# Where the sample's memory attention runs: from the gate units to a third stream beside the prompt's dilated attention

## The chip, the cores and the metric

The kernel runs on one core of a Trainium2 chip. The metric is the device time of one execution in microseconds. TensorE is PE in the views, its weight loads are PEld, VectorE is DVE, ScalarE is ACT, GpSimd is POOL, and SyncE (SP) issues nearly all DMA transfers from one queue.

## The reference, cut to what matters

One layer of a decoder step over a prompt of 1024 tokens and 8 samples of 4 new tokens each. One input projection is split into three groups of heads: retention, dilated sliding-window attention with a rotary embedding, and cross-attention into 256 memory tokens. Each group has a gate; the gated groups go through one output projection and a layer norm. All is fp32. The change touches the memory attention of the samples only:

```python
def _mem_attn(q, k, v):     # q (8, 4 tokens, 4 heads, 128), k and v (8, 256, 4, 128)
    s = jnp.einsum('bthd,bmhd->bhtm', q, k).astype(F32) * (MEM_HD ** -0.5)
    p = jax.nn.softmax(s, axis=-1)
    return jnp.einsum('bhtm,bmhd->bthd', p, v.astype(F32))
```

Each sample has its own `k` and `v` (`cache_mem_k`, `cache_mem_v`, 512 KB each), so sixteen transfers of 512 KB belong to this part.

## The kernel before, in words

The order of the work on every engine is the order in which the program emits it. The trunk of it is a loop over 22 units of the input projection (`UNITS`), two to each name from `mq` to `sg`: memory queries `mq`, memory keys and values `mk` and `mv`, dilated queries and keys `qk`, values `vr`, retention `rq` and `rk`, then the gates `rg`, `mg` and `sg`. A unit takes four blocks of weights (`wr`, 256 KB each); ACT makes the high half `wh` (L172) and DVE the low half `wl` (L175). Its parts are 24 matmuls at L224 each, three (high by high, high by low, low by high) for each of 8 blocks of the contraction, into one tile of the pool `ps_p` (three buffers). Units with the rotary embedding (`qk`, `rq`, `rk`) hold two of these tiles at a time, which DVE and POOL then read.

Between the matmuls, four times in a part, `pump` gives credit to three streams of other work: `fa` (the prompt's attentions), `fb` (the sample's dilated attention) and `fc` (retention, and the sample's memory attention). The table `RATE` holds the credit of each stream by unit. A stream with a whole credit runs its generator to its next `yield`, so what stands there between two yields goes into the program as one piece between two projection matmuls. `drain` runs a stream to its end without any projection between.

In `vr1` to `vr3` (units `vr` 1, `qk` 2, `vr` 2, `rk`, `qk` 3, `vr` 3) `fa` runs the prompt's dilated attention: score matmuls at L523 on `q` and `k` that are read back from memory (`q<-hl_d`), a row operation on DVE (L525), the exponential on ACT (L531), transposes (L573), values (L602). In the rotary units DVE multiplies the projection's tile with a table (L276).

The sample's memory attention is `mem_sample` (L893 to L974). It is added to `fc` when the sample's retention has ended, at the start of `sg` 0, in memory that the retention gave back. It loads `k` tiles (`kv<-in_mem_kT`) into a ring of nine buffers, builds masked queries `msq` (POOL clears them, ACT copies into them), and computes scores in four steps (L930, two samples of different groups of 32 partitions in turns, eight matmuls on 32 columns, one `ps_t` tile for all). A softmax follows, two transposes (L950), four value steps (L960, all in one `ps_o` tile), a product with `own_h` (L964) and a sum (L967) on DVE, a transpose (L970), and a store of `msu` to memory, which the output stage reads as part of the mixed features (`mraw`, times the gate `mg`).

In the second half of `sg` 1 (`MIX_AT`) the program drains `fc`, closes the memory of `mem_sample`, and opens the pools of the output stage there, whose first loads follow. L1498 are the output projection's matmuls. The sample's dilated attention (`fb`) runs in `mg` and `sg`; `dn<-in_swa_kd` (L1058) and the tiles `cl` are its loads. L881 belongs to the sample's retention.

Of the kernel before, what the change touches and what calls it, by code (L numbers as in the profile page):

```python
# [42 lines left out]
MS_Y = 5  # L43
# [26 lines left out]
GT_DEFER = 14  # L70
RT_DEFER = 10
# [26 lines left out]
def trunk_kernel(ctx: ExitStack, tc: tile.TileContext, d):  # L98
# [794 lines left out]
    def mem_sample():  # L893
        kb, vb = {}, {}
        pairs = ((0, 2), (4, 6), (1, 3), (5, 7))
        due = deque((kind, b) for kind in "kv" for pair in pairs for b in pair)

        def load_next():
            if due:
                kind, b = due.popleft()  # L900
                t = msp.tile([128, 1024], F32, tag="kv", name="kv", bufs=9)
                if kind == "k":
                    kb[b] = t.rearrange("p (h m) -> p h m", h=4)
                    load(kb[b], d["mem_kT"][b])
                else:
                    vb[b] = t.rearrange("p (m f) -> p m f", m=2)
                    load(vb[b], d["mem_v"][b])
# [4 lines left out]
        for _ in range(4):  # L912
            load_next()
# [9 lines left out]
        for _ in range(1 + MS_Y):  # L923
            yield
# [18 lines left out]
        for _ in range(2):
            load_next()
            load_next()
            yield
# [8 lines left out]
        o = ps_o.tile([128, 512], F32, tag="o", name="o")  # L955
        for n, pair in enumerate(pairs):
            for mt in range(2):
                for b in pair:
                    g, y = divmod(b, 2)
                    nc.tensor.matmul(o[32 * g:32 * g + 32], lhsT=pm[:, mt, g, y].rearrange("p y r -> p (y r)"), rhs=vb[b][:, mt],  # L960
                                     start=(y == 0 and mt == 0), stop=(y == 1 and mt == 1))
# [787 lines left out]
```

## Time and profile before

| | |
|---|---|
| runs shown | 902.46, 905.25, 922.29 us (median 905.25) |
| profiled execution | 902.89 us, span on the core 901.1 us |
| mean granted clock of TensorE | 0.978 |
| DMA packets | 160.92 MB, mean 179 GB/s |
| chain that ended last | PE 67%, DMA 17%, DVE 5%, SP's queue 4%, ACT 3% |

Times in the rows are microseconds from the start of the span unless they are marked ns. A row of the timeline gives start, duration, engine, line, operation, tile written and tile read, a count, and in brackets how long the engine had stood idle and what ended that. A row of the waits gives the engine, the tile and line that waited, what released it, and the sum, the count and the longest. The granted clock is a share of 2.4 GHz: 0.50 is 1.2 GHz. An fp32 matmul has two records, a matmul of the split halves one.

### The profile page before, as it was taken

What the parts mean: (1) busy time and instruction counts of PE and PEld (TensorE: products, weight loads), DVE (VectorE), ACT (ScalarE), POOL (GpSimd) and SP (SyncE); (2) the same over time, 40 slices, a digit from 0 to 9 for tenths busy, and PEclk for the clock granted to TensorE, in tenths of its full rate; (3) what the DMA queues carried; (4) which work ended last, traced back from release to release, by engine and by line L of the source; (5) the groups of instructions that cost most, each with busy time, mean ns of one, the idle gap of its engine ahead of it and who ended that gap; (6) DMA issues with size and microseconds to landing.
All of it is one profiled execution on the core that took longest, in us unless ns stands there. A gap on an engine that the chain in (4) does not pass through costs nothing.

```text
span 901.1 us, 16168 instructions
## 1 busy us (share of the span) xinstructions
PE 847.5 (94%) x6034; PEld 756.6 (84%) x6034; DVE 456.3 (51%) x1048; ACT 310.4 (34%) x863; POOL 245.7 (27%) x249
## 2 busy tenths in 40 slices
PE   7999999999998999989999999989898889899996
PEld 6999999998997999989998878878775767677776
DVE  5656345145435533555245453585575458545425
ACT  5545234243434433433344444433111442100000
POOL 0004023015123331335012130358450305322201
PEclk9999999999999999999999999999899999899999
DMA  8574324775647544545683326768984868869631
GB/s 262 178 205 140 120 93 130 199 176 108 150 110 160 160 125 133 148 121 126 168 211 84 83 74 208 247 207 294 356 293 151 252 231 241 271 215 307 239 110 56
DMA packets 141646, 160.92 MB, mean 179 GB/s; under 512 B 39232, under 2 KB 102592, under 8 KB 141568
## 3 DMA queue, kind: packets, MB, share of 16 engines
q1 hardware_dynamic: 141568, 159.89, 60.6%
q8 instruction: 48, 0.79, 0.4%
q14 instruction: 30, 0.25, 0.1%
HBM read 120.59 MB, written 39.26 MB: 177 GB/s over the span
## 4 chain that ended last, share of the span: by engine, by line
PE 67%; DMA 17%; DVE 5%; SPq 4%; ACT 3%; issue 2%; POOL 1%; POOLq 0%; DVEq 0%; ACTq 0%
PE pp L224 35%; PE pp L1498 9%; PE s L523 4%; PE o L602 3%; DMA q<-hl_d 3%; SPq L162 3%; DMA wr<-in_w_out 2%; DMA s<-in_xT 2%; DMA dn<-in_swa_kd 2%; PE tp L573 1%; DVE wl L175 1%; PE s L1172 1%; DMA gt_d<-t 1%; PE o L436 1%; PE s L399 1%
## 5 line engine op out<-in xcount | busy, mean ns | idle before, releaser
L224 PE MATMUL pp<-xh,wh 128*128 128x352 f32 x672 | 230.5, 343 | 5.7 <-ACT xh L172 5.3
L224 PE MATMUL pp<-xh,wl 128*128 128x352 f32 x672 | 220.7, 328 | 0.0
L224 PE MATMUL pp<-xl,wh 128*128 128x352 f32 x672 | 220.6, 328 | 0.0
L224 PEld LDWEIGHTS pp<-xh,wh 128*128 128x128 f32 x672 | 130.4, 194 | 16.5 <-issue 9.2
L175 DVE TENSOR_TENSOR wl<-wr,wh 128x512 fp32r<-128x512 f32 (+1 forms) x113 | 91.8, 821 | 87.7 <-ACT wh L172 87.2
L224 PEld LDWEIGHTS pp<-xl,wh 128*128 128x128 f32 x672 | 130.5, 194 | 0.7 <-DVE xl L175 0.5
L224 PEld LDWEIGHTS pp<-xh,wl 128*128 128x128 f32 x672 | 129.8, 193 | 0.3 <-DVE wl L175 0.3
L563 POOL TENSOR_TENSOR pt<-pt,sf 128x256 f32<-128x256 f32 (+1 forms) x128 | 71.3, 593 | 146.2 <-DVE sf L556 130.6
L531 ACT ACTIVATE pt<-pt,sw 128x256 f32<-128x256 f32 (+1 forms) x128 | 59.6, 467 | 83.3 <-DVE sw L525 80.4
L1498 PE MATMUL pp<-wh,mh 128*128 128x512 f32 x192 | 78.9, 411 | 7.7 <-ACT wh L172 6.4
L172 ACT ACTIVATE wh<-wr 128x512 fp32r<-128x512 f32 (+1 forms) x113 | 69.3, 622 | 26.6 <-DMA wr<-in_w_out 22.1
L1498 PE MATMUL pp<-wl,mh 128*128 128x512 f32 x192 | 77.4, 403 | 0.6 <-DVE wl L175 0.5
L1498 PE MATMUL pp<-wh,ml 128*128 128x512 f32 x192 | 77.0, 401 | 0.1
L224 PE MATMUL pp<-wh,xh 128*128 128x256 f32 x256 | 75.0, 293 | 0.5 <-ACT t L172 0.5
L224 PE MATMUL pp<-wl,xh 128*128 128x256 f32 x256 | 72.2, 282 | 0.0
L224 PE MATMUL pp<-wh,xl 128*128 128x256 f32 x256 | 72.0, 281 | 0.0
L523 PE MATMUL s<-k,q 128*128 128x256 f32 (+1 forms) x256 | 56.0, 354 | 12.8 <-DMA q<-hl_d 10.6
L525 DVE CUSTOM_DVE_ANT_0 pt<-s,mask 128x256 f32<-128x256 f32 (+1 forms) x128 | 43.3, 379 | 48.4 <-PE s L523 40.6
L523 PEld LDWEIGHTS s<-k,q 128*128 128x128 f32 x256 | 50.5, 260 | 14.9 <-DVE t L279 5.9
L1071 POOL TENSOR_TENSOR cl<-cl,qb 128x1536 f32<-128x1536 f32 x16 | 56.4, 3542 | 20.2 <-DMA cl<-in_swa_kc 11.2
L1498 PEld LDWEIGHTS pp<-wh,mh 128*128 128x128 f32 x192 | 36.9, 192 | 20.0 <-ACT wh L172 7.7
L1225 POOL TENSOR_TENSOR mraw<-mraw,mg 128x512 f32<-128x512 f32 (+1 forms) x27 | 41.0, 1536 | 45.3 <-DMA mg<-gt_d 44.8
(238 smaller groups left out, 1421.0 us busy)
## 6 DMA issues: line engine op xcount, KB each, us to landing
wr<-in_w_in SPq DMA_DIRECT2D x87, 256.0 KB, 4.0
cl<-in_swa_kc SPq DMA_DIRECT2D x16, 768.0 KB, 6.5
cl<-in_swa_vc SPq DMA_DIRECT2D x16, 768.0 KB, 6.3
hl_d<-hl SPq DMA_DIRECT2D x24, 352.0 KB, 2.9
q<-hl_d SPq DMA_DIRECT2D x32, 256.0 KB, 5.2
tab<-in_tabs SPq DMA_DIRECT2D x18, 352.0 KB, 3.4
gt_d<-t SPq DMA_DIRECT2D x36, 176.0 KB, 5.0
wr<-in_w_out SPq DMA_DIRECT2D x24, 256.0 KB, 5.5
```

The lines of the kernel that those rows point to most:

```text
L162: nc.sync.dma_start(out=out, in_=in_)
L172: nc.scalar.activation(out=out, in_=in_, func=copy, **kw)
L175: (nc.gpsimd if pool else nc.vector).tensor_tensor(out=out, in0=raw, in1=hi.bitcast(F32), op=ALU.subtract)
L224: nc.tensor.matmul(out, lhsT=a, rhs=b, start=(n == 0), stop=(n == 3 * KD - 1))
L523: nc.tensor.matmul(ps[:, out], lhsT=Q[h, b][:, x, q], rhs=K[h][:, k], start=(x == 0), stop=(x == 1))
L525: nc.vector.tensor_tensor_reduce(out=pt[:, out], in0=ps[:, out], in1=mask[:, msk], scale=1.0, scalar=3.0e38, op0=ALU.add, op1=ALU.min, acc ...
L531: nc.scalar.activation(out=pt[:, out], in_=pt[:, out], func=exp, scale=-1.0, bias=st[:, s, i, 0:1], accum_out=st[:, s, i, 1:2])
L563: nc.gpsimd.tensor_tensor(out=pt[:, out], in0=pt[:, out], in1=f[:, 0, 4 * s + i, None].to_broadcast([128, n]), op=ALU.mult)
L602: nc.tensor.matmul(o[64 * g:64 * g + 64, col:col + 128], lhsT=v, rhs=pt[:, at:at + 128], start=g not in begun, stop=last and final[g] == n)
L1071: product(n, K_POOL)(out=pr, in0=pr, in1=qb_t[b][:, None, :].to_broadcast([128, 3, 512]), op=ALU.mult)
L1225: nc.gpsimd.tensor_tensor(out=raw, in0=raw, in1=g, op=ALU.mult)
L1498: nc.tensor.matmul(ps, lhsT=a[:, k], rhs=b[k, c], start=(n == 0), stop=(n == 35))
```

## The change

`mem_sample` is added to `fc` at the start of `vr` 1 (`MS_AT`), with a rate of 0.35 in the six units `vr` 1 to `vr` 3, and `fc` is drained at the start of `rg` 0, where its memory is closed. The memory lies on the other side, above the pool of the rotary tables. The ring has three buffers in place of nine: three tiles are loaded ahead, then two after each step, one yield later. The pair of a step are samples `2g` and `2g+1`, whose results lie in the same 32 partitions, in place of `(0,2)`, `(4,6)`, `(1,3)`, `(5,7)` with results in two groups of 32. Each step has a tile of `ps_p` of its own, which ACT copies out (scores) or DVE multiplies out with `own_h` (values, one operation of 32 partitions for each step). `to_mem`, now `after_rs`, opens nothing any more; `fc.drain()` in `sg` 1 stays.

```diff
+MS_AT = ("vr", 1)
...
-    ("vr", 0): (0.8, 0), ("rq", 0): (0.95, 0), ("vr", 1): (0.65, 0), ("qk", 2): (0.95, 0), ("vr", 2): (0.8, 0), ("rk", 0): (0.7, 0),
...
+    ("vr", 0): (0.8, 0), ("rq", 0): (0.95, 0), ("vr", 1): (0.65, 0, 0.35), ("qk", 2): (0.95, 0, 0.35), ("vr", 2): (0.8, 0, 0.35), ("rk", 0): (0.7, 0, 0.35),
...
     def mem_sample():
-        kb, vb = {}, {}
-        pairs = ((0, 2), (4, 6), (1, 3), (5, 7))
-        due = deque((kind, b) for kind in "kv" for pair in pairs for b in pair)
+        due = deque((kind, b) for kind in "kv" for b in range(8))
+        held = {}
...
-                t = msp.tile([128, 1024], F32, tag="kv", name="kv", bufs=9)
...
+                t = msp.tile([128, 1024], F32, tag="kv", name="kv", bufs=3)
...
-        ps = ps_t.tile([128, 512], F32, tag="t", name="tp")[:, 0:256]
-        for n, pair in enumerate(pairs):
-            for h in range(4):
-                for b in pair:
-                    g, y = divmod(b, 2)
-                    nc.tensor.matmul(ps[32 * g:32 * g + 32], lhsT=qm[:, g, y, h].rearrange("p y h t -> p (y h t)"), rhs=kb[b][:, h],
+        for g in range(4):
+            r = slice(32 * g, 32 * g + 32)
+            ps = ps_p.tile([128, 512], F32, tag="p", name="pp")[r, 0:256]
+            for y in range(2):
+                k = held.pop(("k", 2 * g + y)).rearrange("p (h m) -> p h m", h=4)
+                for h in range(4):
+                    nc.tensor.matmul(ps, lhsT=qm[:, g, y, h].rearrange("p y h t -> p (y h t)"), rhs=k[:, h],
                                      start=(y == 0 and h == 0), stop=(y == 1 and h == 3))
+            acopy(p[r], ps)
             yield
             load_next()
             load_next()
             yield
...
+        for g in range(4):
+            r = slice(32 * g, 32 * g + 32)
+            o = ps_p.tile([128, 512], F32, tag="p", name="pp")[r]
...
+                for mt in range(2):
+                    nc.tensor.matmul(o, lhsT=pm[:, mt, g, y].rearrange("p y r -> p (y r)"), rhs=v[:, mt],
                                      start=(y == 0 and mt == 0), stop=(y == 1 and mt == 1))
...
+            nc.vector.tensor_tensor(out=u4[r], in0=o.rearrange("p (h e) -> p h e", h=4),
+                                    in1=own_h[r, :, None].to_broadcast([32, 4, 128]), op=ALU.mult)
+            yield
+            load_next()
+            load_next()
+            yield
...
+        if (kind, j) == MS_AT:
+            ms_es = ExitStack()
+            msp = pool(ms_es, "msp", 1, side="right")
+            fc.add("ms", mem_sample())
         if (kind, j) == ("rg", 0):
+            fc.drain()
+            close(ms_es)
             close(rope_es)
...
             if u + 1 == len(UNITS) and n == MIX_AT:
                 fc.drain()
-                close(ms_es)
```

PE's order, a score step. Before, in `sg` 0, between projection matmuls of the gate; the numbers behind the names are those of the tiles:

```order
L224 MATMUL pp_7586<-xh_145,wl_7417 128x352
L930 MATMUL tp_7625<-kv_7461,msq_7471 32x256
L930 MATMUL tp_7625<-kv_7463,msq_7471 32x256
L930 MATMUL tp_7625<-kv_7461,msq_7471 32x256
L930 MATMUL tp_7625<-kv_7463,msq_7471 32x256
L930 MATMUL tp_7625<-kv_7461,msq_7471 32x256
L930 MATMUL tp_7625<-kv_7463,msq_7471 32x256
L930 MATMUL tp_7625<-kv_7461,msq_7471 32x256
L930 MATMUL tp_7625<-kv_7463,msq_7471 32x256
L224 MATMUL pp_7634<-xh_145,wh_7103 128x352
```

And now, in `vr` 1:

```order
L224 MATMUL pp_2980<-wh_2369,xh_145 128x256
L224 MATMUL pp_2980<-wl_2370,xh_145 128x256
L224 MATMUL pp_2980<-wh_2369,xl_146 128x256
L929 MATMUL pp_2998<-kv_2783,msq_2791 32x256 x4
L929 MATMUL pp_2998<-kv_2785,msq_2791 32x256 x4
L224 MATMUL pp_2980<-wh_2505,xh_145 128x256
L224 MATMUL pp_2980<-wl_2506,xh_145 128x256
```

The two `kv` tiles no longer take turns, and the step stands in the middle of a projection part, in a tile of that part's pool.

PE's order, the value steps. Before, in the drain of `sg` 1:

```order
L224 MATMUL pp<-xl,wh 128x352
L224 MATMUL pp<-xh,wl 128x352
L950 MATMUL tp<-ident,msp 128x128 x2
L960 MATMUL o<-kv,mspm 32x512 x16
L970 MATMUL tp<-ident,msu_7922 128x128
L224 MATMUL pp<-xh,wh 128x352
L224 MATMUL pp<-xl,wh 128x352
```

And now one of the four, in `rk`:

```order
L224 MATMUL pp_4338<-xl_146,wh_4080 128x352
L224 MATMUL pp_4338<-xh_145,wl_4081 128x352
L959 MATMUL pp_4370<-kv_3678,mspm_2793 32x512 x2
L959 MATMUL pp_4370<-kv_4303,mspm_2793 32x512 x2
L224 MATMUL pp_4338<-xh_145,wh_4195 128x352
L224 MATMUL pp_4338<-xl_146,wh_4195 128x352
```

Sixteen value matmuls in one piece with a transpose ahead and one behind have become four pieces of four, each between projection matmuls.

SP's queue around the loads of `q` in `qk` 2. Before:

```order
L162 DMA so<-st_d_0_97 128x8
L162 DMA k<-hl_d_82 64x1024 x2
L162 DMA q<-hl_d_82 64x2x512 x2
L162 DMA wr<-in_w_in 128x512
L537 DMA st_d_0_99<-sw 128x4x2
L537 DMA st_d_1_100<-sw 128x8
L162 DMA tab<-in_tabs 128x704
```

And now:

```order
L162 DMA k<-hl_d_82 64x1024 x2
L162 DMA q<-hl_d_82 64x2x512 x2
L162 DMA kv<-in_mem_kT 128x1024
L162 DMA kv<-in_mem_v 128x1024
L162 DMA wr<-in_w_in 128x512
L537 DMA st_d_0_99<-sw 128x4x2
L537 DMA st_d_1_100<-sw 128x8
L162 DMA tab<-in_tabs 128x704
```

Two of the sixteen `kv` loads stand directly behind the `q` loads; the first of them is a `k` tile of the fourth score step.

## Rows read from the trace of the kernel before

**Rows 1.** The page's first part, busy time of each engine with its share of the span and the count of instructions.

```profile
PE 847.5 (94%) x6034; PEld 756.6 (84%) x6034; DVE 456.3 (51%) x1048; ACT 310.4 (34%) x863; POOL 245.7 (27%) x249
```

**Rows 2.** Busy time by stage: the stretch, its length, busy us (instructions) of PE, PEld, DVE, ACT and POOL, the granted clock, the DMA share and GB/s. First `vr` 1 to `vr` 3, then `sg` 0 and `sg` 1.

```profile
221.00:448.00 227.00, 220.39 (x1660) 205.74 (x1659) 103.64 (x334) 86.29 (x278) 66.91 (x104) 0.98 0.54 139
634.00:711.00 77.00, 68.33 (x413) 55.58 (x413) 44.67 (x62) 20.02 (x58) 28.29 (x13) 0.93 0.78 262
```

**Rows 3.** The waits of PE from 221 to 448, the heaviest: us, times, longest.

```profile
PE s L523 <- DMA q<-hl_d: 5.8, 2, 3.5
```

**Rows 4.** Records of matmuls. The first three rows group by line and form: duration of one record in ns, shortest, median and longest, and where they lie. The last is four transposes in the timeline.

```profile
L930 PE MATMUL tp<-kv,msq x64: 379/379/603, 653.0 to 674.1; 128*32 128x256 f32 x64
L960 PE MATMUL o<-kv,mspm x32: 592/592/617, 683.4 to 691.1; 128*32 128x512 f32 x32
L573 PE MATMUL tp<-ident,pt x120: 270/272/421, 207.7 to 537.2; 128*128 128x128 f32 x120
210.45 0.60 PE L573 MATMUL tp<-ident,pt 128*128 128x128 f32 x4
```

**Rows 5.** The timeline of PE around one score step in `sg` 0.

```profile
660.46 0.32 PE L224 MATMUL pp<-xl,wh 128*128 128x352 f32 x1
660.62 0.32 PE L224 MATMUL pp<-xh,wl 128*128 128x352 f32 x1
660.87 1.92 PE L930 MATMUL tp<-kv,msq 128*32 128x256 f32 x16
662.72 0.43 PE L224 MATMUL pp<-xh,wh 128*128 128x352 f32 x1
```

**Rows 6.** The timeline of PE and DVE around the drain in `sg` 1.

```profile
681.08 0.32 PE L224 MATMUL pp<-xh,wl 128*128 128x352 f32 x1
...
683.38 2.76 PE L960 MATMUL o<-kv,mspm 128*32 128x512 f32 x18
...
686.84 2.74 PE L960 MATMUL o<-kv,mspm 128*32 128x512 f32 x8 [0.71 <-DMA kv<-in_mem_v]
...
691.75 0.69 DVE L964 TENSOR_TENSOR msu<-o,own_h 128x512 f32<-128x512 f32 x1 [8.54 <-PE o L960]
692.48 1.02 DVE L967 TENSOR_REDUCE msu<-msu 128x128 f32<-128x512 f32 x1
693.64 0.30 PE L970 MATMUL tp<-ident,msu 128*128 128x128 f32 x1 [1.93 <-DVE msu L967]
693.70 0.40 PE L224 MATMUL pp<-xh,wh 128*128 128x352 f32 x1
```

**Rows 7.** Four stretches at half clock, with columns as in rows 2.

```profile
615.90:619.30 3.40, 3.40 (x16) 3.40 (x14) 1.94 (x2) 1.10 (x4) 3.21 (x2) 0.51 0.98 346
646.60:653.40 6.80, 4.85 (x24) 3.87 (x26) 2.60 (x3) 0.62 (x2) 4.87 (x2) 0.50 1.04 353
694.40:697.80 3.40, 3.40 (x14) 3.40 (x13) 2.26 (x5) 0.00 (x0) 0.00 (x0) 0.50 0.15 24
721.70:725.10 3.40, 3.26 (x8) 2.42 (x8) 2.36 (x4) 1.93 (x4) 0.00 (x0) 0.50 0.53 170
```

**Rows 8.** The start of `sg` 0: two rows of PE's timeline, one of SP's, and one of the chain of waits (start, duration).

```profile
644.21 0.32 PE L224 MATMUL pp<-xh,wl 128*128 128x352 f32 x1
...
648.55 0.66 PE L1058 MATMUL sd<-dn,qbd 128*32 128x128 f32 x8 [4.02 <-DMA dn<-in_swa_kd]
...
635.65 1.84 SPq L162 DMA_DIRECT2D kv<-in_mem_kT  x4
...
638.85 9.56 DMA dn<-in_swa_kd
```

**Rows 9.** Loads in the dilated stage: timelines of SP and PE in `qk` 2 and `qk` 3; then the landing of the sixteen `kv` loads in `sg` 0 and 1, and the page's row on the `q` loads (count, KB each, median us to landing).

```profile
281.76 1.25 SPq L162 DMA_DIRECT2D q<-hl_d  x2
283.12 0.54 SPq L162 DMA_DIRECT2D wr<-in_w_in  x1
...
288.22 1.19 PE L523 MATMUL s<-k,q 128*128 128x128 f32 x4 [3.51 <-DMA q<-hl_d]
289.70 0.64 PE L224 MATMUL pp<-xh,wh 128*128 128x352 f32 x1
...
386.59 0.73 PE L523 MATMUL s<-k,q 128*128 128x256 f32 x4 [2.31 <-DMA q<-hl_d]
...
DMA to landing us min/median/max: 4.2/6.8/9.7
...
q<-hl_d SPq DMA_DIRECT2D x32, 256.0 KB, 5.2
```

**Rows 10.** DVE's operation on the projection tile of a rotary unit, grouped by line: ns, and where they lie.

```profile
L276 DVE TENSOR_TENSOR raw<-pp,tab x18: 511/519/527, 67.4 to 417.6; 128x352 f32<-128x352 f32 x18
```

**Rows 11.** The timeline of PE at two places: ahead of the stretch from 615.9, and at the first matmuls of the output projection.

```profile
613.34 1.97 PE L881 MATMUL tp<-rv 32*64 32x128 f32 x16 [1.77 <-ACT rv L172]
...
721.40 0.59 PE L1498 MATMUL pp<-wh,mh 128*128 128x512 f32 x1 [4.93 <-ACT wh L172]
```

**Rows 12.** The waits of SP's queue from 628 to 712, two of them: us, times, longest.

```profile
SPq L151 <- ACT msu L172: 9.5, 1, 9.5
SPq L162 <- DMA ut_d<-msu: 2.4, 1, 2.4
```

More of the change, by code (lines that the diff above doesn't have):

```diff
@@ L42 @@
 RL = 3
-MS_Y = 5
 V_Y = 3
@@ L900, in load_next @@
                 kind, b = due.popleft()
-                t = msp.tile([128, 1024], F32, tag="kv", name="kv", bufs=9)
[L902 to L907, printed above, removed]
+                t = msp.tile([128, 1024], F32, tag="kv", name="kv", bufs=3)
+                load(t.rearrange("p (h m) -> p h m", h=4) if kind == "k" else t.rearrange("p (m f) -> p m f", m=2),
+                     d["mem_kT" if kind == "k" else "mem_v"][b])
+                held[kind, b] = t
         def one(shape, name):
             return msp.tile(shape, F32, name=name)
-        for _ in range(4):
+        for _ in range(3):
             load_next()
@@ L922, in mem_sample @@
                 acopy(qm[:, :, y, h, y, h], mq_s[:, h].rearrange("p (g y t) -> p g y t", y=2, t=4)[:, :, y])
-        for _ in range(1 + MS_Y):
-            yield
-        ps = ps_t.tile([128, 512], F32, tag="t", name="tp")[:, 0:256]
-        for n, pair in enumerate(pairs):
-            for h in range(4):
-                for b in pair:
-                    g, y = divmod(b, 2)
-                    nc.tensor.matmul(ps[32 * g:32 * g + 32], lhsT=qm[:, g, y, h].rearrange("p y h t -> p (y h t)"), rhs=kb[b][:, h],
+        yield
+        p = one([128, 256], "msp")
+        st = stat.tile([128, 16], F32, tag="st", name="st")
+        for g in range(4):
[5 more added lines that the diff above has]
+                    nc.tensor.matmul(ps, lhsT=qm[:, g, y, h].rearrange("p y h t -> p (y h t)"), rhs=k[:, h],
                                      start=(y == 0 and h == 0), stop=(y == 1 and h == 3))
+            acopy(p[r], ps)
             yield
@@ L935, in mem_sample @@
             yield
-        st = stat.tile([128, 16], F32, tag="st", name="st")
-        nc.vector.tensor_reduce(out=st[:, 0:1], in_=ps, axis=AX.X, op=ALU.max)
+        nc.vector.tensor_reduce(out=st[:, 0:1], in_=p, axis=AX.X, op=ALU.max)
         nc.vector.tensor_scalar(out=st[:, 1:2], in0=st[:, 0:1], scalar1=-MEM_SCALE, scalar2=None, op0=ALU.mult)
-        p = one([128, 256], "msp")
-        nc.scalar.activation(out=p, in_=ps, func=exp, scale=MEM_SCALE, bias=st[:, 1:2], accum_out=st[:, 2:3])
+        yield
+        nc.scalar.activation(out=p, in_=p, func=exp, scale=MEM_SCALE, bias=st[:, 1:2], accum_out=st[:, 2:3])
         nc.vector.reciprocal(out=st[:, 3:4], in_=st[:, 2:3])
         nc.vector.tensor_scalar(out=p, in0=p, scalar1=st[:, 3:4], scalar2=None, op0=ALU.mult)
[L943 to L946, printed above, removed]
+        yield
         yield
@@ L954, in mem_sample @@
         yield
[L955 to L960, printed above, removed]
+        u4 = one([128, 4, 128], "msu4")
+        for g in range(4):
+            r = slice(32 * g, 32 * g + 32)
+            o = ps_p.tile([128, 512], F32, tag="p", name="pp")[r]
+            for y in range(2):
+                v = held.pop(("v", 2 * g + y)).rearrange("p (m f) -> p m f", m=2)
+                for mt in range(2):
+                    nc.tensor.matmul(o, lhsT=pm[:, mt, g, y].rearrange("p y r -> p (y r)"), rhs=v[:, mt],
                                      start=(y == 0 and mt == 0), stop=(y == 1 and mt == 1))
+            nc.vector.tensor_tensor(out=u4[r], in0=o.rearrange("p (h e) -> p h e", h=4),
+                                    in1=own_h[r, :, None].to_broadcast([32, 4, 128]), op=ALU.mult)
             yield
-        u4 = one([128, 4, 128], "msu4")
-        nc.vector.tensor_tensor(out=u4, in0=o.rearrange("p (h e) -> p h e", h=4),
-                                in1=own_h[:, :, None].to_broadcast([128, 4, 128]), op=ALU.mult)
+            load_next()
+            load_next()
+            yield
         u1 = one([128, 128], "msu1")
         nc.vector.tensor_reduce(out=u1, in_=u4.rearrange("p h e -> p e h"), axis=AX.X, op=ALU.add)
+        yield
         yield
@@ L1409, in trunk_kernel @@
             close(swa_es)
-            ret_es, cl_es, ms_es = ExitStack(), ExitStack(), ExitStack()
+            ret_es, cl_es = ExitStack(), ExitStack()
             sw1 = pool(cl_es, "sw1", 1)
```

7 lines of the change are left out of this document (2 added, 5 removed), and 2 rows, old and new, of the table RATE.

## The prediction, before the changed kernel had run

> **What bounds the kernel now.** I read the page's busy shares first: TensorE (PE) is busy for 847.5 us of 901.1, and no other engine for more than 456 us [rows 1]. So time can be lost or won in PE's stream, or where PE stands. I then read a table by stage [rows 2]. In 221:448, where the prompt's dilated attention runs beside the projections, PE is busy for 220.4 of 227 us, the DMA share is 0.54 and the rate 139 GB/s. In 634:711 (the gate units `sg0` and `sg1`, where the memory attention of the sample stands) PE is busy for 68.3 of 77 us, the clock is 0.93, and the rate 262 GB/s. The waits of PE in 221:448 name one releaser of weight, the `q` loads, 5.8 us in two waits [rows 3]. The reader is to see that the stage which receives the work has hardly a hole to put it in, while the stage that gives it up has holes.
>
> **What leaves the gate units.** Four score steps: between the L224 matmul before one and the next L224 stand 660.62 + 0.16 (the spacing of L224) to 662.72, that is 1.94 us [rows 5], four times 7.8 us. Then the drain: the last L224 starts at 681.08, the next at 693.70 [rows 6], so 12.5 us hold no projection; in them PE waits for the `v` tiles and for the two DVE operations of 0.69 and 1.02 us. Together 20.3 us. With them go three losses that I tie to this work. After the drain the clock stands at 0.50 from 694.4 to 697.8 [rows 7], where 3.4 us do the work of 1.7. At 644.21 PE waits 4.02 us for a `dn` tile whose load took 9.56 us, issued just after four `kv` loads [rows 8]; and the clock is at 0.50 from 646.6 to 653.4 [rows 7], which costs 3.4 us. 1.7 + 4.0 + 3.4 = 9.1 us. Gone from the gates: 29.4 us.
>
> **What arrives in the dilated stage.** First the price of one step, which is no longer what it was. Before, one score step alternates two samples whose outputs lie at different partitions (groups 0 and 1, or 2 and 3); its 8 matmuls are 16 records. A record of 256 columns lasts 379 ns and one of 512 lasts 592 [rows 4], so 256 columns more take 213 ns; four full-width transposes of 128 columns last 0.60 us, which is a spacing of (0.60 - 0.27)/3 = 109 ns, the same rate [rows 4]. At that rate 16 records after one another would last 15 x 0.213 + 0.379 = 3.58 us. They last 1.92 [rows 5]: two ran side by side. After the change both samples of a step write the same 32 partitions, so nothing runs beside anything: a score step is 1.94 + (3.58 - 1.92) = 3.60 us, a value step of 8 records 7 x 0.427 + 0.592 = 3.58, with the same edges 3.60. Eight steps are 28.8 us; three transposes in two bursts add about 0.9 (an estimate from 0.30 for L970 [rows 6] and the edges). 29.7 us arrive, and since PE there is dense, I count all of it. Both sides so far: 29.7 - 29.4 = +0.3 us.
>
> New waits in the dilated stage, each bounded:
> - The projection pool `ps_p` has three tiles, and a rope unit holds two. At three steps (the third score step in `qk2`, the second value step in `rk`, the last in `qk3`) the step takes the third, and the next half of a rope part then waits for two DVE operations of 0.52 us on the older tile [rows 10]. 0 to 3 x 1.04 = 3.1 us; I take 2, as other PE work stands between at one of them.
> - The fourth score step needs a `k` tile whose load now stands in SP's queue directly behind two `q` loads for which PE already waits 3.51 us, until 288.22 [rows 9]. Issued near 283.1 (where `wr` went out) and landing after 6.8, at most 9.7 us [rows 9], it is there between 289.9 and 292.8; PE asks at 289.7. 0 to 3.1, I take 2.
> - Loads one stream yield ahead of use (at the second value step 24 L224 matmuls lie between, in the order, at a spacing of 0.16 some 4 us of PE's time; at the second score step about the same), against 4.2 us for the quickest landing and 6.8 for the median [rows 9]: 0 to 2.6 each, I take 1 for both, since the first tile of a pair was fetched a step earlier.
> - The second `q` wait near 384 gets one more load of 512 KB in front: 0 to 3, I take 1.
> - What queues behind a late step: ACT's copy of the scores, and on DVE L961 (four of 0.69 at most, against one now), are on nobody's path, because projection tiles rotate through three buffers. POOL's two memsets go from the gates, where POOL waited before them, to `vr1`. The added SP issues (half a microsecond each) hide under PE.
> - Clock: every stretch at 0.50 costs 1.7 us. A step of 3.6 us in which only 32 columns work may be followed by one: 615.9 to 619.3 is such a stretch [rows 7], and what preceded it is 16 narrow matmuls of L881 in 1.97 us after a wait of 1.77 [rows 11]; the earlier narrow steps of 1.92 us had none. 0 to 8 x 1.7 = 13.6; I take one, 1.7, since projections at full width surround each step. The Trainium skill ("TensorE: Matmul & The Clock Gate", Part 1) says that the throttled clock is the default and that a busy array releases it. By that rule alone a step without a hole costs no clock, and this term would be 0; the stretch after L881 leaves it open, because a wait stood there too.
>
> In the gates, with PE's cover gone:
> - DVE is busy for 44.7 us of 77 in 634:711 [rows 2]. Without the memory attention's DVE work (about 2.5) it has 42 us to do while PE's own need shrinks to 77 - 29.4 = 47.6. DVE also waits there for POOL's products, so it may hold projection tiles. 0 to 6, I take 2.
> - SP stood 9.5 us for the result `msu` and 2.4 for its landing before it could fetch `mraw` [rows 12]; PE's later wait of 4.93 us for weights at 721.40 follows from that queue [rows 11]. The mix loads reuse the memory of the `kv` tiles, so both waits go. A gain of 0 to 4.9 + 1.7 (the stretch at 721.7 [rows 7]); I take 2, as those weights also queue behind the mixes and the value cache.
>
> Sum: 0.3 + 2 + 2 + 1 + 1 + 1.7 + 2 - 2 = +8.0 us. The profiled execution took 902.9 us, the median of the runs shown is 905.25. 902.9 + 8 = 911, and with the median's offset 913: I say 912 us.
>
> **Rivals.**
> - *The gates win more than they lose elsewhere.* For it: DMA is at 0.78 in 634:711, and SP's two waits for `msu` stand ahead of the weights. If no new wait comes in the dilated stage and the weights' wait goes with its stretch of clock, the sum is 0.3 - 4.9 - 1.7 = -6.3: 897 us. Against it: 16 loads of 512 KB into a stage where PE already stands for `q`.
> - *A new wait in place of the old, slower than before.* Mechanism: the `kv` tiles (three buffers, two refilled at once) arrive late in the dilated stage, PE stands in the step, and the clock falls after it. Place: the four steps whose second tile is fetched one yield ahead. Price: 2.6 us (median landing less the 4 us of distance) plus 1.7 us for each, 4.3 x 4 = 17, less the 5 us of such waits and clock already in the sum: 912 + 12 = 924, and with a stretch of half clock after the other steps too up to 931. It decides from a landing of about 5 us on. For it: `q` lands in 5.2 us in the median and `kv` in up to 9.7 [rows 9]. Against: at 139 GB/s the stage has room.
> - *The change doesn't double PE's time for a step.* If records to the same 32 partitions overlap after all, the eight steps cost what they did, 13.3 us less: 899. Against it: the spacing of the transposes. The Trainium skill ("TensorEngine Tiling (Array Packing)", Tiling Modes, Key Properties) says that different tiles of the array execute in parallel, and so nothing for two matmuls in one tile; by it this rival is out, and the rows of the alternating step, 1.92 against 3.58, agree.
>
> **How the numbers follow.** Forecast 0.60; gates win 0.18; late tiles 0.17; no doubling 0.05. The likeliest time is 912. Its bounds are 897 (all terms at their low ends with the weights' gain) and 931 (late tiles with clock). From 897 to 930 leaves out about one in ten above and one below. A measurement of this kernel tells some 2% from no change, that is 887 and 923. Below 887 lie only a corner of the second case and of the fourth, 0.04; above 923 most of the late tiles and a corner of the forecast, 0.16; the rest, 0.80, is within.
>
> **What would show it.** Right: L929 bursts of 16 records lasting 3.5 to 3.7 us, L959 bursts of 8 the same; 634:711 shrunk to 47 to 52 us from the first `sg0` matmul to the last of `sg1`; no wait of PE for `dn` near `sg0`; the stage from `vr1` to `vr3` longer by 33 to 40. Wrong: steps of 1.9 us (no doubling); a long PE wait for `kv` in the waits of the dilated stage, or more than three new stretches at half clock (the late tiles); PE standing for DVE in `sg0` (the gates give back what they won); a time under 897 would mean that the transition into the output projection lost its waits altogether.

## The result, and the profile after

The changed kernel took 913.11 us in the median of four runs (910.88 to 914.71), the kernel before 903.86 us on the same chip (four runs); the ratio is 1.0104, 95% interval 1.0057 to 1.0151. Timed once more on another chip it was 1.0114 (1.0075 to 1.0153). It is slower by about one per cent, 9 to 10 us, inside the range of 897 to 930. The prediction took 2% as the least that a measurement of this kernel tells from no change; here the two intervals leave 1 out at half of that. Only runs within 1.5% of the fastest of their kernel enter ratios and means (922.29 us of the kernel before and two runs of `no_mem` at 886 us do not). Chips differ: the median of the kernel before lay between 901.5 and 906.1 us from batch to batch, so experiments are compared by their ratio to the kernel before in the same batch.

The page of the changed kernel, first part, answers to [rows 1]:

```profile
span 911.4 us, 16160 instructions
PE 857.5 (94%) x6034; PEld 756.4 (83%) x6034; DVE 457.7 (50%) x1051; ACT 311.4 (34%) x867; POOL 246.8 (27%) x249
```

PE has as many matmul records as before and is busy 10 us longer. A step now, in the timeline of PE (a score step in `vr` 1 and a value step in `rk`, each with the projection matmul before and after it):

```profile
243.25 0.28 PE L224 MATMUL pp<-wh,xl 128*128 128x256 f32 x1
243.46 3.64 PE L929 MATMUL pp<-kv,msq 128*32 128x256 f32 x16
247.03 0.39 PE L224 MATMUL pp<-wh,xh 128*128 128x256 f32 x1
...
390.20 0.32 PE L224 MATMUL pp<-xh,wl 128*128 128x352 f32 x1
390.46 3.62 PE L959 MATMUL pp<-kv,mspm 128*32 128x512 f32 x8
394.01 0.43 PE L224 MATMUL pp<-xh,wh 128*128 128x352 f32 x1
```

Sixteen records take 3.64 us where the alternating step took 1.92 [rows 5]. The waits of PE from 215 to 476, the whole dilated stage (us, times, longest), are these three and no other:

```profile
PE s L523 <- DMA q<-hl_d: 4.9, 3, 2.9
PE s L523 <- DVE sw L525: 0.8, 1, 0.8
PE o L602 <- DVE ut L614: 0.6, 1, 0.6
```

No wait for a `kv` tile, none for a projection tile, and 4.9 us for `q` against 5.8 [rows 3]. The stages by busy time, columns as in rows 2: `vr` 1 to `vr` 3, `mg` 1, then `sg` 0 and 1.

```profile
221.50:475.00 253.50, 248.81 (x1757) 213.54 (x1757) 108.90 (x343) 89.71 (x297) 68.74 (x106) 0.99 0.60 158
618.80:664.20 45.40, 39.30 (x333) 34.64 (x333) 31.89 (x34) 13.78 (x36) 25.91 (x9) 0.89 0.75 242
664.20:718.50 54.30, 48.98 (x314) 47.05 (x312) 35.50 (x52) 12.86 (x29) 26.98 (x10) 0.99 0.63 203
```

Against [rows 2] the dilated stage grew with PE nearly always busy, and the gates `sg` shrank. The balance by stage, in us, each from the first projection matmul of its first unit to that of the next stage (found by counting the L224 and L251 matmuls in the timeline; one value for each profile taken, those beyond the first from the experiments below; ends read to 0.1 us; `no_mem` has the memory attention left out):

| stretch | before | changed | no_mem |
|---|---|---|---|
| `vr` 1 to `vr` 3 | 226.8, 228.3 | 253.5, 254.7, 253.4 | 224.1 |
| `rg` 0 to `mg` 0 | 145.2, 146.5 | 143.8, 144.3, 143.4 | 145.6 |
| `mg` 1 | 40.7, 42.7 | 45.4, 44.8, 44.4 | 41.0 |
| `sg` 0, `sg` 1 | 76.9, 76.6 | 54.3, 53.2, 56.2 | 52.3 |
| first 24 matmuls of the output projection | 10.7, 11.9 | 15.3, 16.1, 15.0 | 15.0 |

In means: +26.3, -2.0, +3.2, -22.2, +4.2, together +9.5 us. The rest of the output projection and the time ahead of `vr` 1 are each less than 1 us shorter in the mean, so the spans of the profiles differ by 7.9 us. The rest of the output projection alone varies from 176 to 181 us between profiles, so terms of a microsecond or two are within the noise.

### The profile page after: what moved, and what is told of

Its sections match the earlier page's. It is cut to its first block, busy times and chain, and to the rows that moved or that the text cites. A ratio compares the mean times of both kernels' runs of the same rounds, so it can differ in the third digit from the quotient of the medians.

```text
span 911.4 us, 16160 instructions
## 1 busy us (share of the span) xinstructions
PE 857.5 (94%) x6034; PEld 756.4 (83%) x6034; DVE 457.7 (50%) x1051; ACT 311.4 (34%) x867; POOL 246.8 (27%) x249
## 4 chain that ended last, share of the span: by engine, by line
PE 64%; DMA 16%; DVE 7%; issue 3%; ACT 3%; SPq 3%; POOL 2%; POOLq 0%; DVEq 0%; ACTq 0%
PE pp L224 31%; PE pp L1502 9%; PE s L523 4%; DMA q<-hl_d 3%; PE o L602 3%; DMA wr<-in_w_out 2%; SPq L162 2%; PE pp L929 2%; DVE wl L175 2%; DMA s<-in_xT 2%; DMA gt_d<-t 2%; PE pp L959 2%; DMA cl<-in_swa_kc 2%; PE s L1174 1%; PE o L436 1%
## 5 line engine op out<-in xcount | busy, mean ns | idle before, releaser
L224 PE MATMUL pp<-xh,wh 128*128 128x352 f32 x672 | 227.5, 338 | 6.7 <-ACT xh L172 5.6
L224 PE MATMUL pp<-xh,wl 128*128 128x352 f32 x672 | 217.8, 324 | 1.0 <-DVE wl L175 1.0
L224 PE MATMUL pp<-xl,wh 128*128 128x352 f32 x672 | 217.8, 324 | 0.0
L224 PEld LDWEIGHTS pp<-xh,wh 128*128 128x128 f32 x672 | 128.1, 191 | 18.9 <-issue 10.5
L175 DVE TENSOR_TENSOR wl<-wr,wh 128x512 fp32r<-128x512 f32 (+1 forms) x113 | 87.6, 786 | 88.6 <-ACT wh L172 88.1
L224 PEld LDWEIGHTS pp<-xl,wh 128*128 128x128 f32 x672 | 128.4, 191 | 0.6 <-DVE xl L175 0.5
L224 PEld LDWEIGHTS pp<-xh,wl 128*128 128x128 f32 x672 | 127.7, 190 | 1.2 <-DVE wl L175 1.2
L224 PE MATMUL pp<-wh,xh 128*128 128x256 f32 x256 | 75.3, 294 | 0.7 <-ACT t L172 0.7
L224 PE MATMUL pp<-wl,xh 128*128 128x256 f32 x256 | 72.2, 282 | 0.0
L224 PE MATMUL pp<-wh,xl 128*128 128x256 f32 x256 | 72.0, 281 | 0.0
L523 PE MATMUL s<-k,q 128*128 128x256 f32 (+1 forms) x256 | 55.4, 352 | 9.8 <-DMA q<-hl_d 8.4
L1073 POOL TENSOR_TENSOR cl<-cl,qb 128x1536 f32<-128x1536 f32 x16 | 56.1, 3527 | 25.5 <-DMA cl<-in_swa_kc 14.3
L523 PEld LDWEIGHTS s<-k,q 128*128 128x128 f32 x256 | 50.1, 258 | 11.9 <-issue 6.9
L280 POOL TENSOR_TENSOR raw<-raw,t 128x352 f32<-128x352 f32 x18 | 17.3, 962 | 139.1 <-DVE t L278 83.4
```

Of the source, the lines that this page charges most:

```text
L175: (nc.gpsimd if pool else nc.vector).tensor_tensor(out=out, in0=raw, in1=hi.bitcast(F32), op=ALU.subtract)
L224: nc.tensor.matmul(out, lhsT=a, rhs=b, start=(n == 0), stop=(n == 3 * KD - 1))
L523: nc.tensor.matmul(ps[:, out], lhsT=Q[h, b][:, x, q], rhs=K[h][:, k], start=(x == 0), stop=(x == 1))
L1073: product(n, K_POOL)(out=pr, in0=pr, in1=qb_t[b][:, None, :].to_broadcast([128, 3, 512]), op=ALU.mult)
```

## The experiments

**Second and third profiles of both kernels**, without an edit.

> The kernel before, unchanged, profiled a second time. Theory A: the stalls of the gate units that I tied to the memory attention (PE 4.0 us for dn at the start of sg 0, half clock for 6.8 us behind it) belong to the order of the loads and come again within 1 us, and the wait of PE for ACT rv in mg 1 is again below 2.5 us. Rival B: such stalls of this stage are set by when transfers happen to land, and these waits come out otherwise in this execution by 2 us or more, with a span of 897 to 904.

> The changed kernel, unchanged, profiled a second time. Theory A: PE's wait for ACT rv in mg 1 comes again with 5 to 6.5 us and about 10 us of half clock behind it, so it belongs to the new order. Rival B: it was set by when a transfer landed, and is below 3 us or in another place here. Both: time 911 to 915.

> The changed kernel, unchanged, a third profile, timed against the kernel before on another chip. Theory N (the 3.36 us of L808 in mg 1, seen in two of two profiles of this kernel and in none of the two of wc_spread, whose order is the same up to there, depends on when a load of cl lands): it is as likely absent as present here, mg 1 then 40 to 42 us and PE's wait for rv below 3; ratio to the kernel before 1.006 to 1.012. Rival O (it belongs to this program): L808 3.36 us again, PE's wait 5 to 6, mg 1 44 to 46, ratio 1.010 to 1.015.

Before, again: 906.63 us, with a span of 904.8. PE's waits show the `dn` load once more (us, times, longest), and the wait for `rv` is 3.0, not below 2.5:

```profile
PE sd L1058 <- DMA dn<-in_swa_kd: 4.4, 1, 4.4
PE tp L881 <- ACT rv L172: 3.0, 1, 3.0
```

So the `dn` stall that I tied to the memory attention belongs to that order of loads; the two kernels below that leave the memory attention in the gates have it too (3.7 and 4.2 us), and it has no row in any of the three profiles of the changed kernel. The half clock behind it is less steady: 3.4 us here (653.6 to 657.0) and not 6.8. The changed kernel, again: 915.28 us, just above the 911 to 915. The wait for `rv` came as 5.9, 5.0 and 4.3 us in its three profiles, with 10.2, 6.8 and 6.8 us of half clock there; in the third, L808 lasts 3.36 us and `mg` 1 44.4 again, as rival O has it, though the wait is below its 5 to 6; the ratio of 1.0114 fits both forecasts.

**`no_mem`**: the memory attention left out, zeros stored for its result.

```diff
     def mem_sample():
+        ut = msp.tile([128, 4, 8, 4], F32, name="msu")
+        nc.gpsimd.memset(ut, 0.0)
+        store(ut_d[4:8, :, S:T].rearrange("f p t -> p f t"), ut.rearrange("p h b t -> p h (b t)"), wait=ST_DEFER)
+        yield
...
```

> The changed kernel without the sample's memory attention: a zeroed tile is stored in place of its result, no loads of kv, no steps. It prices the work in both places. Theory A (the steps cost their PE time in the dilated stage, nothing else): vr 1 to vr 3 shrinks from 253.5 us to 226 to 228, the gates stay as in the changed kernel, time 884 to 888; the memory attention then cost 17 to 20 us in the gates before, and 26 to 28 after. Rival C (the gates before lost 29 us to it, as I summed): time near 874.

It took 872.21 and 876.92 us against a mean of 904.7 before in the same batch, some 30 us less. Its stages, columns as in rows 2:

```profile
220.30:444.40 224.10, 218.75 (x1659) 204.29 (x1658) 103.83 (x334) 86.27 (x278) 67.31 (x106) 0.99 0.57 141
630.90:683.20 52.30, 48.97 (x314) 46.93 (x312) 34.65 (x53) 12.77 (x29) 26.09 (x10) 1.00 0.63 205
```

It prices the work in both places. In the dilated stage 253.9 - 224.1 = 29.8 us (mean of three profiles of the changed kernel, one of `no_mem`), more than theory A's 26 to 28; PE is busy there 248.81 - 218.75 = 30.1 us less. In `sg` 0 and 1, before, 76.8 - 52.3 = 24.5, between A's 17 to 20 and the 29 of rival C, which was my own sum. The time itself is near C's 874, but 3.4 us of it come from the dilated stage (227.5 in the kernel before) and the rest of the difference from stages that neither theory named. And the first piece of the output projection takes 15.0 us here too, so nothing in the new place makes that loss.

**`side2`**: the two samples of a step lie in different groups of 32 partitions again, in the new place.

```diff
-        due = deque((kind, b) for kind in "kv" for b in range(8))
+        due = deque((kind, b) for kind in "kv" for b in (0, 2, 1, 3, 4, 6, 5, 7))
...
+            for h in range(4):
+                for g in gs:
+                    nc.tensor.matmul(ps[32 * g:32 * g + 32], lhsT=qm[:, g, y, h].rearrange("p y h t -> p (y h t)"), rhs=k[g][:, h],
+                                     start=(h == 0), stop=(h == 3))
+            if y == 0:
+                acopy(p[r], ps[r])
+            else:
+                nc.vector.tensor_tensor(out=p[r], in0=p[r], in1=ps[r], op=ALU.add)
...
```

> The changed kernel with the two samples of a step in different groups of 32 partitions, (0,2), (1,3), (4,6), (5,7), in turns; the second step of a group is added to the first on DVE (two additions for scores, two for values, one multiplication with own_h for all). Same place, rate, three buffers. Theory A (outputs in the same partitions make the steps long): score bursts of 16 records last 1.9 us and not 3.64, value bursts of 8 records 1.9 and not 3.62, so 8 x 1.7 = 13.7 us less, 898 to 902. Rival D (the steps' length is not what costs, the loads and the clock are): 910 to 915.

**`side4`**: half tiles, four samples of four groups in a step.

```diff
+                t = msp.tile([128, 512], F32, tag="kv", name="kv", bufs=7)
...
+            y, x = divmod(n, 2)
+            k = [held.pop(("k", y, x, g)).rearrange("p (h m) -> p h m", h=2) for g in range(4)]
+            for h in range(2):
+                for g in range(4):
+                    nc.tensor.matmul(ps[32 * g:32 * g + 32], lhsT=qm[:, g, y, 2 * x + h].rearrange("p y h t -> p (y h t)"), rhs=k[g][:, h],
+                                     start=(h == 0), stop=(h == 1))
...
```

> The changed kernel with half tiles (256 KB each, seven buffers) and four samples in a step, one in each group of 32 partitions, in turns; the four partial results are added on DVE (three additions of 256 and three of 512 columns, one multiplication with own_h). 32 loads in place of 16, the same bytes. Theory A (time goes by how many groups run side by side): a score burst of 16 records lasts 1.0 us (4 x 0.213 + 0.17) in place of 3.64 in the changed kernel, a value burst of 8 about 1.0, so 8 x 2.6 = 21 us less than the changed kernel: 892 to 897, and 7 below side2. Rival D (at most two run side by side): bursts of 1.9 us, 901 to 906, as side2.

A score step of each in PE's timeline, first `side2`:

```profile
241.13 1.92 PE L930 MATMUL pp<-kv,msq 128*32 128x256 f32 x16
```

and `side4`, with a value step behind it:

```profile
245.40 1.07 PE L931 MATMUL pp<-kv,msq 128*32 128x256 f32 x16
351.12 1.06 PE L962 MATMUL pp<-kv,mspm 128*32 128x512 f32 x8
```

The same 16 records take 3.64 us on one group, 1.92 on two in turns, 1.07 on four in turns. `side2` is at 0.998 of the kernel before (0.9937 to 1.0023; 903.6 us), a little more than the forecast 898 to 902; `side4` at 0.9901 (0.9866 to 0.9936; 896.48 us). Theory D falls twice. But not all of it arrives. `side4` should hold 29.8 - 8 x 2.6 = 9 us more than `no_mem` in the dilated stage and holds 19 (columns as in rows 2):

```profile
222.40:465.50 243.10, 232.52 (x1757) 209.41 (x1757) 109.59 (x345) 88.98 (x293) 69.03 (x106) 0.97 0.63 164
```

The waits of PE in this stretch of `side4`:

```profile
PE s L523 <- DMA q<-hl_d: 8.3, 3, 4.3
PE o L602 <- DVE ut L614: 1.5, 1, 1.5
```

PE reaches the `q` loads earlier and waits 8.3 us for them, 3.4 more than in the changed kernel; in the whole stretch it stands 243.10 - 232.52 = 10.6 us and not 4.7, and the clock is at 0.97 and not 0.99. The shorter the steps, the more of the old waits stand open again (4.9, 5.6 and 8.3 us for `q` with one, two and four groups).

**`gates_same` and `gates4`**: the old place, with one group and with four groups to a step.

```diff
-        pairs = ((0, 2), (4, 6), (1, 3), (5, 7))
+        pairs = ((0, 1), (2, 3), (4, 5), (6, 7))
```

> The kernel before with the pairs (0,1), (2,3), (4,5), (6,7), so both samples of a step write the same 32 partitions, in the old place. Theory A: score bursts of 3.6 us and not 1.92, 6.7 us more in sg 0; the value steps 3.6 us each and not 1.9, of which a part hides in the waits for v: 4 to 7 more; together 915 to 920. Rival G (the gates have slack that swallows it, PE there waits for DVE and loads in any case): 903 to 910 with the bursts long all the same.

```diff
-        pairs = ((0, 2), (4, 6), (1, 3), (5, 7))
+        quads = ((0, 2, 4, 6), (1, 3, 5, 7))
...
-            for h in range(4):
-                for b in pair:
+            for h in range(4):
+                for b in quad:
...
```

> The kernel before, the memory attention in its old place, with four samples of four groups in a step, (0,2,4,6) and (1,3,5,7), in turns: two score steps of 32 records in place of four of 16, two value pieces in place of four. It tells what the place does apart from the packing. Theory A (the place matters once the packing is equal): score steps of 2.1 us, twice, in place of 1.92 four times, 3.5 us less, value steps hidden behind the loads of v; 900 to 904, so the same packing is worth 4 to 8 us more in the dilated stage (side4 896.5). Rival K (the packing alone is the gain, the place nothing): 894 to 899.

A score step in PE's timeline of `gates_same`, then of `gates4`:

```profile
663.97 3.64 PE L930 MATMUL tp<-kv,msq 128*32 128x256 f32 x16
```

```profile
649.23 2.34 PE L930 MATMUL tp<-kv,msq 128*32 128x256 f32 x32
```

The two `sg` units of `gates_same`, then of `gates4`, columns as in rows 2:

```profile
635.20:719.00 83.80, 75.89 (x414) 59.16 (x413) 45.59 (x61) 18.59 (x55) 26.57 (x13) 0.96 0.72 243
```

```profile
630.90:704.90 74.00, 62.48 (x413) 51.85 (x412) 42.48 (x59) 17.18 (x51) 28.66 (x12) 0.98 0.78 265
```

The one-group step costs 7 us more in `sg` (83.8 against 76.8), as the score bursts say (4 x 1.7), and the whole is at 1.0051 (1.0014 to 1.0088; 908.40 us). That lies in rival G's range, but the gates did not swallow the score steps. My 915 to 920 was too much because the value steps did not get longer; all four of `gates_same`:

```profile
691.22 8.86 PE L960 MATMUL o<-kv,mspm 128*32 128x512 f32 x32
```

One after another, 32 records would take 31 x 0.427 + 0.592 = 13.8 us. They stand in one piece here, each step writes another group of 32 partitions than the step before it, and records of successive steps ran side by side although their order does not take turns. In the kernel before they take about 8.4 us (683.38 to 691.75 [rows 6]), the waits for `v` included.

Four groups save 2.8 us in `sg` and nothing that can be measured in the whole: 1.0019 (0.9977 to 1.0060). So rival K, the packing alone, falls, and so does the 3.5 us of theory A; that the same packing is worth more in the dilated stage, theory A's other half, holds. By packing, new place against old: with four groups to a step 0.990 against 1.002, and the intervals do not overlap; with two, `side2` against the kernel before, 0.998, which is no difference that can be measured; with one, 1.010 against 1.005, with intervals that overlap. So the place is worth about 1.2% with the densest packing only (`side2` and `side4` also add partial results on DVE, and `side4` has half tiles, so these pairs differ in more than the place). And the packing that the change gave up cost 1.2% in the new place, 1.0104 against 0.998, with intervals that do not overlap.

**`norm_pool`**: what stands behind the wait for `rv` in `mg` 1. The timeline of the changed kernel there, on POOL, DVE and PE:

```profile
638.00 0.55 POOL L793 TENSOR_TENSOR rs<-rs,nhalf 128x1 f32<-128x1 f32 x1
638.51 10.43 POOL L1073 TENSOR_TENSOR cl<-cl,qb 128x1536 f32<-128x1536 f32 x3
638.58 3.36 DVE L808 SCALAR_TENSOR_TENSOR mv<-mv,rs 128x1 f32<-128x1 f32 x1 [3.74 <-POOL rs L793]
642.88 2.88 PE L881 MATMUL tp<-rv 32*64 32x128 f32 x16 [5.95 <-ACT rv L172]
```

and the stretch at half clock there, columns as in rows 2:

```profile
638.60:648.80 10.20, 5.92 (x27) 5.59 (x28) 8.57 (x6) 4.61 (x15) 10.06 (x3) 0.50 0.92 309
```

L808 works on one column and takes 3.36 us. It starts 0.07 us after POOL's next multiplication of `cl`, and it ends when the first of these three (10.43 / 3 = 3.48 us each) ends. ACT's scaling waits for it, `rv` stands behind that on ACT, PE's L881 behind `rv`, and the clock is at 0.50 for 10.2 us. The edit lets POOL do L808's work itself:

```diff
+            nc.gpsimd.tensor_tensor(out=mv[:, 0:n, 1], in0=mv[:, 0:n, 0], in1=neg, op=ALU.mult)
+            nc.gpsimd.tensor_tensor(out=mv[:, 0:n, 1], in0=mv[:, 0:n, 1], in1=rs[:, 0:n], op=ALU.mult)
-        nc.vector.scalar_tensor_tensor(out=mv[:, 0:n, 1], in0=mv[:, 0:n, 0], scalar=-1.0, in1=rs[:, 0:n], op0=ALU.mult, op1=ALU.mult)
```

> The changed kernel with one DVE operation of the sample's retention norm (L808, 0.16 us before, 3.36 us in both profiles of the changed kernel) done by two small operations on POOL. Theory E (L808 stands while POOL's 3.46 us multiplication of cl runs beside it, and PE's wait for rv in mg 1 comes from there): PE's wait for rv in mg 1 falls from 5.0 to 5.9 us to 2 to 3.5, mg 1 from 45 to 41 to 43 us, the whole by 2 to 5 us. Rival F (the late work is before L808, in the loads of cl): wait and mg 1 stay, 912 to 916.

Its rows at the same place:

```profile
636.13 0.19 POOL L809 TENSOR_TENSOR mv<-mv,neg 128x1 f32<-128x1 f32 x1
636.39 0.19 POOL L810 TENSOR_TENSOR mv<-mv,rs 128x1 f32<-128x1 f32 x1
636.55 3.44 POOL L1079 TENSOR_TENSOR cl<-cl,qb 128x1536 f32<-128x1536 f32 x1
...
637.46 1.97 PE L887 MATMUL tp<-rv 32*64 32x128 f32 x16 [1.59 <-ACT rv L172]
```

POOL goes on to the next multiplication at once, as in the changed kernel, and PE waits 1.59 us and not 4.3 to 5.9; `mg` 1 is 40.7 us. Theory E holds for the wait and for `mg` 1. The ratio is 1.0063 (1.0026 to 1.0100), some 4 us below the changed kernel's, but the intervals overlap, so the gain of the whole is not shown.

**`wc_spread`**: ACT's twelve copies at the start of the output projection in three pieces.

```diff
-            for c in range(0, 6, 2):
+            for n in range(V_LEAD):
+                load_cl(d["swa_vc"], n)
+                c = 2 * n
...
+                for _ in range(V_Y):
+                    yield
-            for n in range(V_LEAD):
-                load_cl(d["swa_vc"], n)
-                for _ in range(V_Y):
-                    yield
```

> The changed kernel with ACT's twelve copies to wc (3.74 us in one piece at the start of the output projection) in three pieces of four, apart. Theory H (they stand in front of the weights' wh on ACT, and so PE's first long wait in the output projection, 5.3 to 6.2 us, comes from them): the wait falls to 2.5 to 4 us. Rival I (the weights land late in any case, 7 us from issue): the wait stays at 5 to 6.5.

> wc_spread once more, timed. Its first look was 906.4 us, with mg 1 at 41.7 us and PE's wait for rv at 1.9, which its edit does not touch. Theory L (the edit shortens the first piece of the output projection from 15 to 16 us to 12, and the wait for rv is set by chance of landing): first piece 12 to 13 again, median 909 to 912. Rival M (both were chance): first piece 15 to 16, median 912 to 915.

PE's waits around the start of the output projection in the changed kernel:

```profile
PE pp L1502 <- ACT wh L172: 6.2, 1, 6.2
PE pp L1502 <- DVE t L304: 3.3, 1, 3.3
PE pp L224 <- DVE t L304: 1.1, 1, 1.1
PE pp L224 <- DVE wl L175: 1.0, 1, 1.0
```

The end of the longest one in the timeline of `wc_spread`, on PE and ACT:

```profile
726.77 0.80 PE L1502 MATMUL pp<-wh,mh 128*128 128x512 f32 x1 [5.33 <-ACT wh L172]
726.09 0.63 ACT L172 ACTIVATE wh<-wr 128x512 fp32r<-128x512 f32 x1 [7.58 <-DMA wr<-in_w_out]
```

Theory H falls: the wait for `wh` is 5.33 us all the same, and ACT itself stands 7.58 us for the load of those weights, as rival I has it. The piece up to there was 12.0 and 12.4 us in the two profiles and not 15 to 16, so the edit did shorten something ahead of it. What, stays open: PE is also busy only 6.1 and 7.2 us in that piece and not 7.9 to 8.6, with its clock at 0.89 and 0.77 and not 0.71 to 0.75. The whole is at 1.0095 (1.0050 to 1.0141; 908.93 us), which cannot be told from the changed kernel. The wait for `rv` was 1.9 and 1.3 us in the two profiles of this kernel, although the order up to there is that of the changed kernel. Its timeline on DVE and POOL shows what differed:

```profile
637.84 0.16 DVE L808 SCALAR_TENSOR_TENSOR mv<-mv,rs 128x1 f32<-128x1 f32 x1 [2.92 <-POOL rs L793]
638.59 10.39 POOL L1073 TENSOR_TENSOR cl<-cl,qb 128x1536 f32<-128x1536 f32 x3 [0.78 <-DMA gt_d<-t]
```

Here POOL had to wait another 0.78 us, and L808 slipped in before it. Less than a microsecond decides over some 4. L808 of the sample's norm lasts 0.16 us in `side2`, `side4`, `no_mem` and the kernel before too. Why the changed kernel fell on the bad side three times of three and this one on the good side twice stays open.

**`side4_all`**: `side4` with the edits of `norm_pool` and `wc_spread`.

> side4 with the two edits of norm_pool and wc_spread. Theory L (the first piece of the output projection was 3 us shorter in wc_spread because of the edit, and side4 has that 15.6 us piece too; the norm edit finds nothing to win, as side4's wait for rv is 1.6 us): 892 to 895. Rival M (the 3 us of wc_spread were chance): 895 to 899, as side4.

888.77 us, below both forecasts, and 0.9879 of the kernel before (0.9826 to 0.9932; 901.45 us in this batch). That is faster than both kernels, but it cannot be told from `side4` alone (0.9901). The first piece of the output projection was 12.5 us against 15.6, as theory L has it; the dilated stage, which the two edits do not touch, was 239.7 against 243.1.

## Why the prediction came out right

The forecast was 912 us, 8 above the profiled execution of before; it became 913.1. That the total came within 2 us is luck: two errors of 11 to 13 us had opposite signs. The price of a step was right for its own reason.

- **The price of a step: right.** I took 3.58 us for 16 records in one group, from the rate of a wider matmul and of a transpose; 3.64 and 3.62 were measured. The 29.7 us that arrive are close to the 29.8 between `no_mem` and the changed kernel, and `side2` and `side4` show that the shared 32 partitions are the cause. The Trainium skill ("TensorEngine Tiling (Array Packing)", Theoretical Speedup) gives up to a factor of four for stationary matrices of 32 columns; 3.64 / 1.07 = 3.4 agrees.
- **New waits in the dilated stage: wrong.** I summed 2 + 2 + 1 + 1 + 1.7 = 7.7 us for projection tiles, late `kv` tiles, the second `q` wait and the clock, and forecast a stage longer by 33 to 40. It grew by 26.3. Projection tiles and `kv` tiles have no row among the waits. The fourth score step's tile, issued at 294.65 behind `q`, landed 5.5 us later at 300.2, when the step had just begun. PE had stood for `q` until 299.20, and the first half of the step works on its other tile, fetched earlier:

```profile
294.65 0.59 SPq L162 DMA_DIRECT2D kv<-in_mem_kT  x1
299.20 0.70 PE L523 MATMUL s<-k,q 128*128 128x128 f32 x4 [2.94 <-DMA q<-hl_d]
300.16 5.33 PE L929 MATMUL pp<-kv,msq 128*32 128x256 f32 x16
```

The landing of the sixteen `kv` loads of the changed kernel:

```profile
DMA to landing us min/median/max: 3.8/5.4/7.9
```

The median is 5.4 us and not the 6.8 of the gates [rows 9], which I had carried over from a stage with 262 GB/s to one with 158. The distance was larger than the 4 us I took, too: the late load of the second score step went out at 250.44, and the step began at 258.76. At the second value step the tile came just in time: issued at 367.66, it landed 4.5 us later, and its half of the step began at 373.2.

The clock term was wrong. The stretches at half clock of this stage, two in the kernel before and one in the changed kernel (columns as in rows 2):

```profile
288.20:291.60 3.40, 3.38 (x13) 3.40 (x14) 1.76 (x3) 1.31 (x2) 2.87 (x5) 0.50 0.75 37
387.20:390.60 3.40, 3.40 (x17) 3.02 (x17) 1.64 (x6) 1.09 (x4) 0.25 (x1) 0.50 0.09 3
300.70:304.10 3.40, 3.40 (x10) 1.44 (x9) 1.73 (x6) 0.99 (x4) 0.16 (x1) 0.50 1.19 261
```

Both of the kernel before begin where a wait at L523 has ended [rows 9]; the one of the changed kernel stands in the fourth score step, behind its wait of 2.94 us (so this step lasts 5.33), and the seven other steps of 3.6 us had none. The other profiles have 6.8 us before, 6.8 and 3.4 after, so no stretch was added. And this stage had lost some 3 us to waits and clock before the change (227.5 against 224.1 in `no_mem`; the same stage of `gates_same` and `gates4` took 226.8 and 225.2). That the steps now fill part of this is argued from the rows, not shown by itself.
- **What the gates give: too much by 12 us.** I had 29.4 gone, 2 back for DVE, 2 more gained in front of the output projection, so 29.4 in all; -22.2 - 2.0 + 3.2 + 4.2 = -16.8 was measured from `rg` 0 to the first piece of the output projection. Of the 20.3 us of steps and drain and 9.1 us of tied losses, `no_mem` finds 24.5 in `sg`. The `dn` wait did go, in all three profiles. The row 634:711 was to shrink to 47 to 52 us and shrank to 53.2 to 56.2.
- **The wait in front of the output projection: wrong sign.** I had a gain of 2, because SP's waits for `msu` were ahead of those weights [rows 12]. They went, and PE still waits 6.2 us for `wh` (4.9 in [rows 11]); `wc_spread` shows that the weights' own load is what ends last. The first 24 matmuls, before and changed:

```profile
710.74:721.40 10.66, 5.74 (x26) 4.33 (x24) 4.00 (x6) 2.35 (x6) 3.02 (x3) 1.00 0.72 234
718.46:733.74 15.28, 8.59 (x25) 6.24 (x25) 5.73 (x9) 6.74 (x20) 3.85 (x3) 0.72 0.74 230
```

More than half of the 4.2 us lost here is the clock: the same matmuls keep PE busy for 8.59 us at 0.72 and not 5.74 at 1.00 (7.9 and 7.9 in the other two profiles of the changed kernel, 5.8 in the other of the kernel before). The piece starts behind a wait of 3.3 us for DVE. With the gates short, PE now stands for DVE at the end of `sg` (3.3, 1.1 and 1.0 us); I had placed this DVE term in `sg`, with 2, and these waits are part of its 54.3 us.
- **`mg` 1: not foreseen.** 3.2 us, through L808 beside POOL. No step of the prediction looks at a stage that the change does not touch.
- **The rivals.** The late tiles did not come, for the reasons above, although the landing of 5.4 us was past the 5 from which I let it decide. Of the gates that win more than they lose elsewhere, the first condition came, no new wait in the dilated stage; the second, a shorter way into the output projection, did not. That the doubling might not be there is excluded by the rows of the step.

## What to carry to other kernels

Price a moved step by its packing in the new place, not by its old duration: in the denser stage the step on one group cost 1.2% of the whole against the step on two. Work put into a stage with little idle time costs its full busy time; work taken out of a stage that several engines share gave back less here than the hole it left, because something else (DVE, the load of the weights, and the clock behind these waits) then set the time. A run with the work left out shows both prices at once, and shows errors that cancel in the sum.

## What the runs showed of the hardware

Four matmuls of 32 stationary columns on four groups of output partitions ran side by side: 16 fp32 records of 256 columns in 1.07 us, against 1.92 on two groups and 3.64 on one. I had expected the two, and not been sure of four. The order need not take turns for it: in the drain of `gates_same` steps of eight records, each on one group, overlapped with the next step on another group, 32 records of 512 columns in 8.86 us and not 13.8.

A DVE operation of 0.16 us (L808, which reads `mv` and `rs`, both in SBUF) stood for 3.36 when a POOL multiplication had started 0.07 us before it, and took 0.16 when it came first (`wc_spread`); another operation on DVE ran at its usual length beside the same POOL work (L1052, a reduction with one input):

```profile
642.53 1.74 DVE L1052 TENSOR_REDUCE Ec<-cl 128x24 f32<-128x1536 f32 x1
```

The Trainium skill ("SBUF — State Buffer", Who interferes with whom) says that a VectorE instruction with two inputs in SBUF contends with a GpSimd instruction that reads SBUF, that the one which starts first keeps the shared ports for its whole length, and that reductions never contend. The rows of L1073, L808 and L1052 agree.
